# Weight splits and modulation sums on whole pieces of 1024 columns instead of two halves of 512

## The chip, the cores and the metric

One core of a Trainium2 chip runs the whole program. The metric is the device time of one execution in microseconds (us), as the median over several runs of the same kernel. Beside the times there is one profiled execution, from which all rows below come. Engines go by these names: PE is TensorE's matmul, PEld its weight load, DVE VectorE, ACT ScalarE, SP SyncE, which issues the loads of the weights.

## The reference

Two blocks of a network run one after the other over 256 tokens of width 1024, all in fp32. Block 1 has one layer: an attention with low-rank projections beside a pooling branch, a cross attention over a memory, and a mixture of 32 experts. Block 2 has two layers, each with a feed-forward part, a token-mixing part (two kinds of attention, gates and an output product) and a second feed-forward part. Cut to what matters here:

```
mod = silu(c) @ ada_w[l] + ada_b[l]             # nine vectors of 1024 per layer
sh1, sc1, g1, ... = split(mod, 9)
n1 = rms_norm(h, g) * (1 + sc1) + sh1
h  = h + 0.5 * g1 * ((silu(n1 @ wg) * (n1 @ wu)) @ wd)       # feed-forward, d_ff = 2816
```

`c` is one row of 1024 values, so each modulation vector is a matrix of 1024 x 1024 times one vector. `n1 @ wg`, `n1 @ wu` and `@ wd`, and all the projections of the attentions, are dense products of the 256 tokens with a weight matrix.

## The kernel before

**Precision.** The array multiplies in a reduced fp32 form (`float32r`). To keep fp32's accuracy, both factors of a dense product are split in two parts, x = xh + xl and w = wh + wl, and three products are summed: xh wh + xh wl + xl wh (`mm3`, lines 430 to 434). So each weight that is loaded has to go through two elementwise steps before TensorE can use it: ScalarE writes `whi`, the rounded copy (line 205), and VectorE writes `wlo` = w - whi (line 212).

**Pieces.** All weights come from DRAM in pieces of 128 rows x 1024 columns of fp32, 512 KB each (a few are narrower), in the order of their use. The class `Stream` (from line 164) keeps that order. There are three kinds. S is a dense product's weights, split as above: 445 pieces. A is 128 outputs of a modulation vector: 144 pieces (2 layers x 9 vectors x 8). R is the experts' weights, which are used as they come and are not split. `plan` (line 338) places the A pieces among the S pieces; in the phases of block 2 (feed-forward, mixing, feed-forward, for each layer) there are 36, 16, 28, 28, 12 and 8 of them (`ADA_N`, line 43). A feed-forward stage has 66 S pieces: 11 blocks of 256 hidden columns with four pieces of gate and up weights and two of down weights each.

**Slots.** A piece that has been loaded takes one of 4 slots (tag `raw`, tile `w`); the two parts take one of 8 slots each (tags `hi` and `lo`, tiles `whi` and `wlo`). The raw slot is free when VectorE has made `wlo`, or has summed an A piece; the slots of `whi` and `wlo` are free when TensorE has done its last product with the piece. `pump` (line 216) puts out, at each step of the program, all loads, copies and subtractions that the slots allow; a copy comes no sooner than 2 pieces (`LAG`) after its load, a subtraction no sooner than 2 after its copy, unless the piece is due. Each engine runs its instructions in an order that is fixed when the program is built. So a copy that waits for its load holds up everything behind it on ScalarE, and a subtraction everything behind it on VectorE.

**Halves.** `_hi` and `_lo` (lines 199 and 207) work on columns 0 to 511 and 512 to 1023 of a piece in two instructions each. The first half's subtraction needs only the first half's copy. An A piece (`ada_piece`, line 615) is multiplied with the row silu(c) and summed along the columns in two instructions as well: the first starts from the bias and leaves its sum in `apart`, the second starts from `apart` and leaves the result in a column of `acolt`. The products themselves are not wanted and go to `ajunk`, a bf16 tile.

**Gate vectors.** Every third modulation vector is needed along the rows. `ada_finish` (lines 626 to 637) writes it to DRAM by columns (`gate`, line 636) and reads it back to all 128 rows (`growt`, line 637). Both are issued by SyncE, in order with the weights' loads.

**A feed-forward stage** (`ffn`, line 1519). For each block i of hidden columns and each tile t of 128 tokens: `gu_part` multiplies with four pieces; `act` has ScalarE compute `si` = silu(gate) (line 1543) and VectorE the product `pr` (line 1545); `tp` transposes `pr` on TensorE (line 438) and splits it in `hTh` (ScalarE, line 502) and `hTl` (VectorE, line 503); `down` multiplies these with two pieces into `facc`. In TensorE's order, `tp` of block i comes right behind `down` of block i - 1, and `down` of block i one round later.

**Mixing and norms.** In `mix2` (line 1648) two attentions run as units of scores, softmax, transposes and products, with dense products as filler between them. The norms' steps (`NormMod`, from line 2034) run inside the neighbouring products with a raised priority (`urgent`, line 1940), which puts them 30 instructions ahead of where they stand in the program.

The lines that the change and the prediction's steps touch: 205 and 212 (splits), 623 (modulation sums), 192 (loads), 636 and 637 (gates), 502 and 503, 1543 and 1545 (feed-forward), 1736 and 1837 (attention).

Of the kernel before, what the change touches and what calls it, by code (L numbers as in the profile page):

```python
# [10 lines left out]
F32 = mybir.dt.float32  # L11
# [34 lines left out]
# ---------------------------------------------------------------------------  # L46
# constants that depend on shapes alone
# ---------------------------------------------------------------------------
def _constants():
# [4 lines left out]
    # moe: [t', t] = 1 where t' < t  # L54
# [7 lines left out]
    # block 1 attention: chunk mask rows, added as two more rows of the contraction  # L62
# [6 lines left out]
    c["maskrows"] = np.stack([mq, mk], axis=1)  # [2, (q,k), S]  # L69
# [9 lines left out]
    )  # [p, g, t', tok]  # L79
# [3 lines left out]
    # block 2: axial angles, distances  # L83
# [4 lines left out]
    cs = np.stack([np.cos(ang), np.sin(ang)], axis=1).astype(np.float32)  # [S, 2, sec, 16]  # L88
# [8 lines left out]
# ---------------------------------------------------------------------------  # L97
# layout of the inputs
# ---------------------------------------------------------------------------
# [48 lines left out]
class Piece:  # L148
# [7 lines left out]
    def half(self, i):  # L156
        """Columns 512 i to 512 i + 511 of a piece of kind R."""
        if self.tag is None and len(self.place[0]) == 2:
            return self.place[0][i]
        raw = self.place[0][0] if self.tag is None else self.raw  # L160
        return raw[:, i * 512:(i + 1) * 512]


class Stream:
    """The weights in the order of their use: loads run ahead as far as slots are free. Kind S is split
    into two float32r parts ahead of its use; R is used as it is; A goes into a
    modulation vector."""

    def __init__(self, K, order):
        self.K = K  # L170
        self.rec = order is None
        self.order = [] if order is None else order
        self.pos = self.i_dma = self.i_hi = self.i_lo = self.clock = 0
        self.live = {"raw": 0, "hi": 0, "lo": 0}
        self.cap = {"raw": N_RAW, "hi": N_HI, "lo": N_HI}
        self.hold = math.inf  # from this piece on, no splits yet but those that must
        self.extra = []  # more places for pieces of kind R: its tiles, whether it can be used again
        self.deferred = []
        self.ada_done = {}
# [14 lines left out]
    @staticmethod  # L194
    def _halves(p):
        """In two, so that short steps of other chains get in between sooner."""
        return [slice(c, min(c + 512, p.n)) for c in range(0, p.n, 512)]

    def _hi(self, p):
# [4 lines left out]
        for sl in self._halves(p):  # L204
            K.nc.scalar.activation(p.hi[:, sl], p.raw[:, sl], AF.Copy)  # L205

    def _lo(self, p):
# [3 lines left out]
        for sl in self._halves(p):  # L211
            K.nc.vector.tensor_sub(p.lo[:, sl], p.raw[:, sl], p.hi[:, sl].bitcast(F32))  # L212
# [3 lines left out]
    def pump(self, upto=-1, raw=N_RAW):  # L216
        """Puts out the steps that can run by now, and those of the pieces up to a position anyhow."""
# [43 lines left out]
    def hold_after(self, n):  # L261
        """Holds back the splits after those of the next n pieces of kind S."""
# [46 lines left out]
    # modulation vectors: a piece for each 128 rows  # L309
# [28 lines left out]
def plan(order):  # L338
    """Places the pieces of the modulation weights among the others."""
# [11 lines left out]
    at = []  # (position, piece)  # L351
# [7 lines left out]
    # of the others, so many in each phase of the second block: the vector engine has more else to do in some  # L359
# [27 lines left out]
class Kernel:  # L387
# [28 lines left out]
    def load(self, dst, src):  # L416
        """Behind what is traced so far on its queue's engine, so not ahead of weights that are due before."""
        self.tc.keep_in_program_order(self.nc.scalar.dma_start(dst, src))
# [21 lines left out]
    def rsqrt(self, y, v, t, scale, n=1):  # L440
        """y = scale * v ** -0.5 (all [P, n]; t is scratch): a first guess (within 3.4%) from the bits; then
        y <- ((v y^2)^2 + c1 v y^2 + c0) y, the minimax step within that range, which takes b v^-0.5 to
        (b^5 / k) v^-0.5 within 2.6e-5; then Newton's y <- (v y^2 - 3 g^2) y, from g v^-0.5 to -2 g^3 v^-0.5."""
# [20 lines left out]
    def warm(self, n, after=None, tag="mm"):  # L464
        """Products whose results nobody reads, so that the array's clock is not gated down while it has to wait."""
# [14 lines left out]
    def ss(self, dst, src, scale=1.0):  # L480
        """dst [P, 1] = sum of the squares of scale * src (up to 512 columns)."""
# [6 lines left out]
    def rstd(self, st, width, two=True):  # L488
        """(sum of squares / width + eps) ** -0.5 from the sums in st[:, 0:2]."""
# [8 lines left out]
    def split_T(self, hi, lo, src, gain=None):  # L498
        """hi/lo float32r of src * gain, gain per partition."""
# [8 lines left out]
    def transpose_split(self, hi, lo, src, kts, t, k0=0):  # L508
        """hi/lo[:, k0 + k, t's tokens] = src[:, k's columns] ^ T."""
# [29 lines left out]
    def dense(self, name, hi, lo, kt, width, src, evac, cb=512, tag="acc", outer=None, mid=None, pre=None, post=None):  # L539
        """A generator: for each block of columns, out[t] = x[t] @ w, then evac(t, b, out). Groups of  # L540
        outer blocks take all of one tile of tokens before the other; else the tiles take turns at each
        piece. mid follows the first group's first tile; pre(t, b) each evac; post(0)
        precedes the last tile's evac. Yields True between groups."""
# [66 lines left out]
    def c_silu(self):  # L610
        """silu(c) along the rows."""
# [3 lines left out]
    def ada_piece(self, l, m, i, raw):  # L615
        """128 outputs of a vector, by columns, from the transposed weights."""
# [3 lines left out]
        part = self.small(1, "apart")  # L620
        junk = self.ct([P, 512], mybir.dt.bfloat16, name="ajunk")
        for sl, acc, out in ((slice(0, 512), self.gcol("ada_b", (l * 9 + m) * 8 + i), part), (slice(512, D), part, r)):
            self.nc.vector.tensor_tensor_reduce(out=junk, in0=raw[:, sl], in1=self.c_row[:, sl], scale=1.0, scalar=acc,  # L623
                                                op0=ALU.mult, op1=ALU.add, accum_out=out)

    def ada_finish(self, l, m):
# [5 lines left out]
        elif m % 3 == 2:  # L632
            # along the rows, by way of DRAM
# [10 lines left out]
    def gain_row_pe(self, name, tile):  # L644
        """The same without a transfer for each partition; tile() gives places of 512 columns."""
# [15 lines left out]
    # =======================================================================  # L661
# [34 lines left out]
    def mixer(self, nrm):  # L696
# [3 lines left out]
        with self.phase("mix1") as pool:  # L700
# [14 lines left out]
            cs = self.ct([P, 2, 2, 16], name="cs")  # [p, (cos, sin), t, 16]  # L715
            rs = nrm.rs

            def tables():
                """rope tables of the positions"""
# [58 lines left out]
            def rope(x, t, heads, o1, o2):  # L778
                """x: [P, heads, 32] view, in place."""
# [39 lines left out]
            # pooling: d^T = u^T band, y^T = w^T d^T  # L819
# [9 lines left out]
            # gates and the pooling branch run between the steps of the attention  # L829
# [83 lines left out]
            def values(hp, p0, p1):  # L913
# [13 lines left out]
                # transposed, the two heads in their halves of the columns of the array  # L927
# [43 lines left out]
    def cross(self, nrm, pool):  # L971
# [26 lines left out]
        def to_T(dst, src, t, b):  # L998
            """dst[:, 4b.., t] = src ^ T, src [P, 512]."""
# [74 lines left out]
        # what the experts' phase starts with  # L1074
# [16 lines left out]
        # the output product, one tile of tokens after the other; the first two heads' half runs early  # L1091
# [56 lines left out]
    def moe(self, nrm, pool):  # L1148
# [16 lines left out]
        # the weights also use memory that other things need before or later  # L1165
# [20 lines left out]
        def route(t):  # L1186
            """Scores of the groups and experts, the chosen two and their weights."""
# [16 lines left out]
            def first_max(oh, x, n, m):  # L1204
                """oh = 1 at the first of x's greatest, m = the greatest."""
# [18 lines left out]
            # weights: 1 and exp(m2 - m1) over their sum, times 1 / sum of the groups' exponentials  # L1224
# [20 lines left out]
        def rank(t):  # L1245
            """Ranks: earlier tokens of the same expert; beyond 1000 for tokens of others."""
# [34 lines left out]
        # gather: columns of x^T by slot  # L1281
# [4 lines left out]
        def overflow():  # L1286
            # weights of the tokens beyond an expert's slots
# [6 lines left out]
        def gather(q):  # L1294
            """A generator: G and the products of each tile of tokens."""
# [8 lines left out]
            def mm(o, k2, t):  # L1304
                # the bank's first product clears the bits of both halves
# [38 lines left out]
        def slot_weights(q):  # L1344
            """The slots' rows scales, and their weights times these."""
# [14 lines left out]
        # G transposed  # L1360
# [103 lines left out]
    def overflow(self, xnT, cwo, rs, cnti, pool):  # L1464
        """The experts over all tokens, with the weights of those that found no slot; skipped where
        all did."""
# [52 lines left out]
    def ffn(self, l, w, nrm, nxt):  # L1519
        nc, S_ = self.nc, self.S  # L1520
        A, V, T = nc.scalar, nc.vector, nc.tensor
        with self.phase(f"ffn{l}{w}") as pool:
# [53 lines left out]
            # the first two and the last take all of one tile of tokens before the other  # L1576
# [71 lines left out]
    def mix2(self, l, nrm, nxt):  # L1648
# [3 lines left out]
        with self.phase(f"mix2{l}") as pool:  # L1652
# [26 lines left out]
            def tables():  # L1679
                """The distances and slopes; the cosines and sines with the gains (and the scale of the scores)."""  # L1680
# [44 lines left out]
            def rope(out, o, n, t, j):  # L1725
                """out = the rotated heads of o (PSUM) with their gains, not yet normalized; the sums of squares."""
# [457 lines left out]
```

## Time and profile before

| | before |
|---|---|
| runs: median (lowest to highest of 3) | 1723.43 us (1722.06 to 1725.42) |
| profiled execution: span from its first to its last instruction | 1710.4 us |
| around the span, to the runs' median | 13.0 us |
| instructions: copies `whi`, subtractions `wlo` | 888 and 888 |
| instructions: modulation sums | 288, each with a read of the accumulator |
[...]

The profiled execution's own time is told as its span; the runs are timed around it, so the 13.0 us are what lies before the first and after the last instruction. The profile's page gives busy time for each engine. Its views group instructions by line, list what each engine waited for (`A <- B`: A sat idle until B was done), and give the busy time in stretches of the span. The stretches used below: block 1's attentions 0 to 300 us, the experts 300 to 525, then block 2: feed-forward 535 to 735, mixing 735 to 945, feed-forward 945 to 1130 and 1130 to 1335, mixing 1335 to 1505, feed-forward 1505 to 1695.

### The profile page before, as it was taken

The numbers are of one execution on the slowest core, as the hardware profiler recorded it, in microseconds if no ns is written. First come the engines' busy times: TensorE is split into PE (matmuls) and PEld (weight loads), VectorE is DVE, ScalarE is ACT, GpSimd is POOL, SyncE is SP. The second block draws the span as 40 slices with busy tenths as digits, with TensorE's granted clock in tenths as the row PEclk, the third lists the DMA queues.
The fourth block names the chain that finished last, engine by engine and source line by source line (L and its number), as shares of the span: only waits on it lengthen the run. The fifth ranks groups of instructions, "written<-read, shape, count | busy, mean of one in ns | idle before, by whom it ended". The sixth has DMA issues, their size and how long they took to land.

```text
span 1710.4 us, 22657 instructions
## 1 busy us (share of the span) xinstructions
PE 1600.0 (94%) x7704; PEld 1197.0 (70%) x7704; DVE 1139.6 (67%) x2633; ACT 817.2 (48%) x1752; POOL 0.2 (0%) x4
## 2 busy tenths in 40 slices
PE   8999999788879989889999899999998999999998
PEld 7878887333115767667778787877876877878886
DVE  7878756111008878687889777778775788886664
ACT  5655642111006434366765444455443768474442
POOL 0000000000000000000000000000000000000000
PEclk9999999989999999999999999999999999999999
DMA  7667759799996898755576887858787744756663
GB/s 247 206 216 280 231 181 360 273 409 408 408 408 222 302 262 289 248 197 196 167 239 199 254 283 256 273 183 301 257 267 184 222 166 160 244 185 212 223 211 89
DMA packets 128645, 424.10 MB, mean 248 GB/s; under 512 B 21098, under 2 KB 23434, under 8 KB 128524
## 3 DMA queue, kind: packets, MB, share of 16 engines
q1 hardware_dynamic: 122160, 414.00, 70.5%
q10 hardware_dynamic: 6364, 8.60, 1.7%
q8 instruction: 62, 1.02, 0.2%
q14 instruction: 59, 0.48, 0.1%
HBM read 421.47 MB, written 1.07 MB: 247 GB/s over the span
## 4 chain that ended last, share of the span: by engine, by line
PE 33%; DMA 29%; DVE 11%; ACT 3%; issue 3%; SPq 0%; DVEq 0%; ACTq 0%
DMA w<-in_w_dram 19%; DMA w<-in_wm_dram 6%; DVE wlo L212 5%; PE d L432 4%; PE d L434 4%; PE d L433 4%; PE ps L433 3%; PE ps L434 3%; PE ps L432 3%; DVE ajunk L623 3%; PE ps L438 2%; DMA gate<-acolt 2%; PE facc L432 2%; PE facc L433 2%; PE facc L434 2%
## 5 line engine op out<-in xcount | busy, mean ns | idle before, releaser
L205 ACT ACTIVATE whi<-w 128x512 fp32r<-128x512 f32 (+1 forms) x888 | 513.6, 622 | 460.3 <-DMA w<-in_w_dram 314.3
L212 DVE TENSOR_TENSOR wlo<-w,whi 128x512 fp32r<-128x512 f32 (+1 forms) x888 | 574.3, 682 | 159.9 <-ACT whi L205 156.3
L432 PE MATMUL ps<-whi,xh 128*128 128x512 f32 x704 | 278.8, 396 | 0.8 <-ACT xh L2080 0.5
L433 PE MATMUL ps<-wlo,xh 128*128 128x512 f32 x704 | 275.3, 391 | 0.8 <-DVE wlo L212 0.7
L434 PE MATMUL ps<-whi,xl 128*128 128x512 f32 x704 | 275.1, 391 | 0.0
L432 PE MATMUL d<-whi,xh 128*128 128x512 f32 (+3 forms) x528 | 206.4, 391 | 0.2 <-ACT xh L2080 0.2
L433 PE MATMUL d<-wlo,xh 128*128 128x512 f32 (+3 forms) x528 | 203.5, 385 | 1.1 <-DVE stat L457 1.1
L434 PE MATMUL d<-whi,xl 128*128 128x512 f32 (+3 forms) x528 | 203.2, 385 | 1.0 <-DVE xl L503 1.0
L623 DVE CUSTOM_DVE_ANT_0 ajunk<-w,c_row,cols 128x512 bf16<-128x512 f32 x144 | 107.5, 746 | 95.5 <-DMA w<-in_w_dram 95.5
L433 PEld LDWEIGHTS ps<-wlo,xh 128*128 128x128 f32 x704 | 132.5, 188 | 28.2 <-DVE wlo L212 2.0
L432 PEld LDWEIGHTS ps<-whi,xh 128*128 128x128 f32 x704 | 132.4, 188 | 28.0 <-ACT xh L2080 1.2
L434 PEld LDWEIGHTS ps<-whi,xl 128*128 128x128 f32 x704 | 132.3, 188 | 28.0 <-DVE xl L2081 0.4
L432 PE MATMUL facc<-whi,hTh 128*128 128x512 f32 x352 | 144.9, 412 | 4.4 <-ACT hTh L502 4.4
L434 PE MATMUL facc<-whi,hTl 128*128 128x512 f32 x352 | 140.7, 400 | 1.1 <-DVE hTl L503 1.0
L433 PE MATMUL facc<-wlo,hTh 128*128 128x512 f32 x352 | 140.9, 400 | 0.0
L432 PEld LDWEIGHTS d<-whi,xh 128*128 128x128 f32 x528 | 100.2, 190 | 21.2 <-issue 3.6
L434 PEld LDWEIGHTS d<-whi,xl 128*128 128x128 f32 x528 | 100.3, 190 | 20.1 <-DVE xl L503 1.7
L433 PEld LDWEIGHTS d<-wlo,xh 128*128 128x128 f32 x528 | 100.4, 190 | 18.4 <-DVE wlo L212 1.7
L623 DVE CUSTOM_DVE_ANT_0 ajunk<-w,c_row,apart 128x512 bf16<-128x512 f32 x144 | 107.7, 748 | 3.1
L1399 PE MATMUL ps<-w,xg 128*32 128x512 f32 x472 | 86.3, 623 | 14.3 <-DMA w<-in_wm_dram 7.9
L432 PEld LDWEIGHTS facc<-whi,hTh 128*128 128x128 f32 x352 | 68.3, 194 | 19.4 <-ACT hTh L502 6.6
L434 PEld LDWEIGHTS facc<-whi,hTl 128*128 128x128 f32 x352 | 68.0, 193 | 17.3 <-DVE hTl L503 2.6
(405 smaller groups left out, 1855.2 us busy)
## 6 DMA issues: line engine op xcount, KB each, us to landing
w<-in_w_dram SPq DMA_DIRECT2D x578, 512.0 KB, 4.5
w<-in_wm_dram SPq DMA_DIRECT2D x163, 512.0 KB, 9.3
adaacc<-in_wm_dram SPq DMA_DIRECT2D x16, 512.0 KB, 10.2
xf<-in_wm_dram SPq DMA_DIRECT2D x16, 256.0 KB, 9.6
growt<-gate SPq DMA_DIRECT2D x6, 512.0 KB, 5.7
w<-in_w_dram SPq DMA_DIRECT2D x6, 384.0 KB, 3.7
growt<-in_rows_dram ACTq DMA_DIRECT2D x4, 512.0 KB, 6.0
bg<-in_rows_dram ACTq DMA_DIRECT2D x8, 256.0 KB, 4.7
```

The source lines that it names most:

```text
L205: K.nc.scalar.activation(p.hi[:, sl], p.raw[:, sl], AF.Copy)
L212: K.nc.vector.tensor_sub(p.lo[:, sl], p.raw[:, sl], p.hi[:, sl].bitcast(F32))
L432: mm(out, lhsT=xh, rhs=wh, start=start, stop=False)
L433: mm(out, lhsT=xh, rhs=wl, start=False, stop=False)
L434: mm(out, lhsT=xl, rhs=wh, start=False, stop=stop)
L438: self.nc.tensor.transpose(out, in_, self.ident[:k, :k])
L623: self.nc.vector.tensor_tensor_reduce(out=junk, in0=raw[:, sl], in1=self.c_row[:, sl], scale=1.0, scalar=acc, op0=ALU.mult, op1=ALU.add, a ...
L1399: T.matmul(gu[e * CAP:(e + 1) * CAP, :], lhsT=xg[j // 2][:, k, c:c + CAP], rhs=p.half(e % 2), start=(k == 0), stop=(k == KD - 1), tile_pos ...
```

## The change

A piece's copy is one instruction over all its columns, and its subtraction another; `_halves` is gone. An A piece is summed in one instruction that starts from the bias and leaves its result in the column of `acolt`. Its products, in fp32, overwrite the piece itself; `ajunk` and `apart` are gone. All comments are taken out as well.

```diff
-    @staticmethod
-    def _halves(p):
-        return [slice(c, min(c + 512, p.n)) for c in range(0, p.n, 512)]
...
     def _hi(self, p):
...
         p.hi = K.wpool.tile([P, PIECE], F32R, name="whi", tag="hi", bufs=N_HI)
-        for sl in self._halves(p):
-            K.nc.scalar.activation(p.hi[:, sl], p.raw[:, sl], AF.Copy)
+        K.nc.scalar.activation(p.hi[:, :p.n], p.raw[:, :p.n], AF.Copy)
 
     def _lo(self, p):
...
         p.lo = K.wpool.tile([P, PIECE], F32R, name="wlo", tag="lo", bufs=N_HI)
-        for sl in self._halves(p):
-            K.nc.vector.tensor_sub(p.lo[:, sl], p.raw[:, sl], p.hi[:, sl].bitcast(F32))
+        K.nc.vector.tensor_sub(p.lo[:, :p.n], p.raw[:, :p.n], p.hi[:, :p.n].bitcast(F32))
...
     def ada_piece(self, l, m, i, raw):
...
         r = self.ada_accs[(l, m)][:, i:i + 1]
-        part = self.small(1, "apart")
-        junk = self.ct([P, 512], mybir.dt.bfloat16, name="ajunk")
-        for sl, acc, out in ((slice(0, 512), self.gcol("ada_b", (l * 9 + m) * 8 + i), part), (slice(512, D), part, r)):
-            self.nc.vector.tensor_tensor_reduce(out=junk, in0=raw[:, sl], in1=self.c_row[:, sl], scale=1.0, scalar=acc,
-                                                op0=ALU.mult, op1=ALU.add, accum_out=out)
+        self.nc.vector.tensor_tensor_reduce(out=raw, in0=raw, in1=self.c_row, scale=1.0,
+                                            scalar=self.gcol("ada_b", (l * 9 + m) * 8 + i),
+                                            op0=ALU.mult, op1=ALU.add, accum_out=r)
```

## Rows read from the trace of the kernel before

**Rows 1.** The page, part 1: engine, busy us (share of span), instructions.

```profile
PE 1600.0 (94%) x7704; PEld 1197.0 (70%) x7704; DVE 1139.6 (67%) x2633; ACT 817.2 (48%) x1752; POOL 0.2 (0%) x4
```

**Rows 2.** What TensorE waited for: us in total, times, longest us.

```profile
PE ps L438 <- DVE pr L1545: 35.4, 14, 6.6
...
PE ps L433 <- DVE wlo L212: 0.7, 2, 0.5
```

**Rows 3.** Stretches: length; busy us of PE, PEld, DVE, ACT, POOL; clock; DMA share; GB/s.

```profile
600.00:735.00 135.00, 115.80 (x500) 92.73 (x500) 95.71 (x210) 51.07 (x103) 0.00 (x0) 0.95 0.83 267
...
1548.00:1677.00 129.00, 129.00 (x584) 106.30 (x583) 76.65 (x145) 60.48 (x120) 0.00 (x0) 1.00 0.66 202
```

**Rows 4.** What ScalarE waited for from 600 to 735 us.

```profile
ACT whi L205 <- DMA w<-in_w_dram: 69.0, 30, 9.4
```

**Rows 5.** Loads of weights from 600 to 735 us: count, KB each, us to landing.

```profile
w<-in_w_dram SPq DMA_DIRECT2D x65, 512.0 KB, 5.0
```

**Rows 6.** What SyncE's queue waited for from 600 to 735 us.

```profile
SPq L637 <- DMA gate<-acolt: 17.9, 2, 9.3
```

**Rows 7.** A stretch behind the first long wait; columns as in rows 3.

```profile
616.80:623.50 6.70, 4.20 (x11) 3.43 (x12) 6.10 (x13) 3.14 (x8) 0.00 (x0) 0.50 0.87 303
```

**Rows 8.** Groups by line and shape: count, busy us, mean ns, idle before.

```profile
L205 ACT ACTIVATE whi<-w 128x512 fp32r<-128x512 f32 x877 | 510.0, 625 | 459.9 <-DMA w<-in_w_dram 313.9 <-PE ps L434 47.2 <-PE facc L434 34.8
...
L205 ACT ACTIVATE whi<-w 128x256 fp32r<-128x256 f32 x6 | 2.4, 404 | 0.0
...
L212 DVE TENSOR_TENSOR wlo<-w,whi 128x512 fp32r<-128x512 f32 x877 | 570.0, 685 | 159.9 <-ACT whi L205 156.3 <-PE d L434 0.9
...
L623 DVE CUSTOM_DVE_ANT_0 ajunk<-w,c_row,cols 128x512 bf16<-128x512 f32 x144 | 107.5, 746 | 95.5 <-DMA w<-in_w_dram 95.5
...
L994 DVE TENSOR_TENSOR mem<-mem,growt 128x1024 f32<-128x1024 f32 x2 | 2.4, 1217 | 0.0
```

**Rows 9.** Timeline, one S piece: start, length, engine, line, count, [idle before].

```profile
646.84 1.15 ACT L205 ACTIVATE whi<-w 128x512 fp32r<-128x512 f32 x2 [2.51 <-DMA w<-in_w_dram]
...
647.50 1.29 DVE L212 TENSOR_TENSOR wlo<-w,whi 128x512 fp32r<-128x512 f32 x2 [0.84 <-ACT whi L205]
```

**Rows 10.** Timeline of VectorE ahead of a late `pr`: sum, subtraction, `pr`.

```profile
1047.26 0.75 DVE L623 CUSTOM_DVE_ANT_0 ajunk<-w,c_row,cols 128x512 bf16<-128x512 f32 x1 [1.78 <-DMA w<-in_w_dram]
...
1048.74 1.29 DVE L212 TENSOR_TENSOR wlo<-w,whi 128x512 fp32r<-128x512 f32 x2
...
1049.94 0.75 DVE L1545 TENSOR_TENSOR pr<-ps,si 128x256 f32<-128x256 f32 x2
```

**Rows 11.** The same ahead of another: two pieces' copies, then `pr`.

```profile
615.67 2.43 ACT L205 ACTIVATE whi<-w 128x512 fp32r<-128x512 f32 x4 [3.65 <-DMA w<-in_w_dram]
...
618.83 0.42 DVE L1545 TENSOR_TENSOR pr<-ps,si 128x256 f32<-128x256 f32 x1
```

**Rows 12.** The same ahead of a third: half a copy, then `pr`.

```profile
655.46 0.63 ACT L205 ACTIVATE whi<-w 128x512 fp32r<-128x512 f32 x1 [2.82 <-DMA w<-in_w_dram]
...
656.72 0.42 DVE L1545 TENSOR_TENSOR pr<-ps,si 128x256 f32<-128x256 f32 x1
```

**Rows 13.** Timeline of ScalarE at a feed-forward stage's end.

```profile
1126.03 0.63 ACT L205 ACTIVATE whi<-w 128x512 fp32r<-128x512 f32 x1 [2.28 <-DMA w<-in_w_dram]
1126.56 0.36 ACT L502 ACTIVATE hTh<-ps 128x256 fp32r<-128x256 f32 x1
```

**Rows 14.** Timeline of VectorE in the mixing: a lone half, then `zqa`.

```profile
806.58 0.68 DVE L212 TENSOR_TENSOR wlo<-w,whi 128x512 fp32r<-128x512 f32 x1
807.18 0.68 DVE L1736 TENSOR_TENSOR zqa<-zqa,rtmp 128x512 f32<-128x512 f32 x1
```

**Rows 15.** A stretch, columns as in rows 3; then `ajunk`'s instructions alone (DVE).

```profile
903.00:946.00 43.00, 42.96 (x204) 34.74 (x203) 39.90 (x92) 26.94 (x55) 0.00 (x0) 1.00 0.62 197
...
903.00:946.00 43.00, 7.45 (x10) 1.00 0.62 197
```

## The prediction, made before the changed kernel was run

> **What bounds the kernel now.** I read the page's busy shares first. TensorE is busy for 1600.0 of 1710.4 us and VectorE for 1139.6 [rows 1], so only about 110 us of the span are TensorE's to win, and VectorE is no bound on average. The list of what TensorE waited for then says which engine's lateness matters: the splits themselves almost never do (0.7 us on `wlo` in the whole span), while the transposes of the gated products `pr` waited 35.4 us in 14 places [rows 2]. All 14 lie in the four feed-forward stages of block 2. The busy time by stretch shows that a stage can also be free of any stall: from 1548 to 1677 us TensorE is busy all 129 us, whereas from 600 to 735 it is idle for 19 us [rows 3]. In that second stretch ScalarE's splits stood 69.0 us waiting for weights [rows 4], so the stream of weights is late there, and `pr` is late only because its `si` and its own product stand behind late splits in two in-order queues. Two things make the stream late. A piece's slot (four of them) is filled again only after VectorE has read it, and a load takes 5.0 us [rows 5]; and SyncE, which issues the loads, stood 17.9 us waiting for the gate vectors' scatter before it could go on [rows 6]. [...]
>
> So what is to be asked of this change is not how much busy time it saves, but how long a chain takes from a landed piece to a free slot and to `pr`.
>
> **Prices of the new instructions.** The copy on ScalarE takes 625 ns for 512 columns and 404 for 256 [rows 8], 221 ns for 256 more, so 625 + 2 x 221 = 1067 ns for 1024 (an estimate). On VectorE a two-operand step over 1024 columns is in the trace: 1217 ns against 685 for 512 [rows 8], 532 ns more. The modulation sum over 512 columns takes 746 ns [rows 8]; with 532 more a whole one takes 1.28 us. That it writes fp32 in place instead of bf16 into a junk tile shows in no row; I take nothing for it, since 512 columns take 532 ns in the step that writes fp32 too; at worst it is another 0.5 us on each of 144, 77 us of VectorE's time, at best nothing.
>
> In a queue the start to the next start counts. A lone half holds VectorE for 0.60 us (806.58 to 807.18) [rows 14], 0.085 less than its duration, so a whole subtraction holds it for 1.13 us against 1.20 for two halves: 0.07 saved on each of 443 pieces that have two halves, 31 us in all. The two halves of a sum hold it for 1.48 us (1047.26 to 1048.74) [rows 10], a whole one for 1.28 - 0.07 = 1.21: 0.27 saved 144 times, 39 us. ScalarE saves about 0.08 a piece, 35 us. None of these 105 us lies on the path by itself; TensorE's work covers them, and the instructions, loads and their queue are otherwise unchanged: one load a piece as before, no wait added.
>
> [...]
>
> **1. From landing to a free slot.** Now: a copy starts at 646.84, its first half releases the subtraction at 647.50, which ends 1.29 us later [rows 9], 1.95 us in all. Two engines work on two halves at once. With whole pieces the subtraction can only start when all of the copy is done: 1.067 + 0.03 + 1.217 = 2.31 us, 0.36 more. A modulation piece is free 0.27 us earlier. From 600 to 735 us, 65 loads [rows 5] in 135 - 17.9 us are 1.80 us a load, so 7.2 us a slot, of which 5.0 are the load. With about two split pieces to one modulation piece (66 to 36 in this stage's order) the round gets (2 x 0.36 - 0.27) / 3 = 0.15 us longer, 0.037 us a load: +2.4 us for 65. Ends: 0 if loads get faster because fewer are in flight; +5.9 if the sums always stand behind a longer subtraction (0.36 on each). I take +2.4: that is what the chains give without either. In the other feed-forward stages part of the copies wait for slots of `whi` that TensorE frees, so the longer chain is covered; without that cover the 2 x 94 loads of the next two stages (66 split pieces and 28 modulation pieces each) would cost +7.0.
>
> **2. From landing to `pr`.** With today's order kept, the 14 waits end as follows. Five have a sum and then both halves of a subtraction ahead of `pr` [rows 10]: 0.27 + 0.07 earlier, -1.7 us. Five have two pieces' copies and subtractions ahead [rows 11]: the second subtraction can't begin at its copy's middle, some +0.3 each, +1.5. One has a copy's half, `si`, a subtraction's half, `pr` [rows 12]: `si` fits between the halves now, and later `pr` would start at 655.46 + 1.067 + 0.03 + 1.13 = 657.69 instead of 656.72, +0.97. Two have half a sum or half a subtraction ahead, where a whole one would be, +0.9; one stands behind a backlog, -0.1. At the stages' ends three transposed products `hTh` stand behind one half of a copy [rows 13], +0.43 each, +1.3, and one behind a sum, -0.3. Sum +2.6. Ends: -3 if the new order puts `pr` ahead of the subtractions, +7 if it always comes behind.
>
> **3. Attention.** Three of TensorE's waits there stand behind a lone half of a subtraction, as `zqa` does [rows 14]. A whole one in its place holds VectorE 1.13 instead of 0.60 us: 3 x 0.53 = +1.6. At best the split moves behind the step, -1.8; the other end is the second rival.
>
> **4. Lead before a gate's transfer.** From 903 to 946 us VectorE is busy for 39.90 of 43 us, five sums among that [rows 15] (ten halves). There its speed does set how far the splits run ahead of TensorE when SyncE next stalls. Five sums save 1.3 us: -1.3, between 0 and the first rival.
>
> Sum: 2.4 + 2.6 + 1.6 - 1.3 = +5.3 us on the profiled span of 1710.4, 1715.7. The runs' median is 1723.43, 13.0 us above the span for what lies around it, so **1728.7 us**, 0.3% slower. A measurement of this kernel can tell about 0.2%, 3.4 us, from no change.
>
> **Rivals.** *VectorE's relief becomes lead: faster.* 70 us less on VectorE let the splits run one piece further ahead before the gates' transfers. A piece is 12 matmuls at 129 / 584 = 0.22 us [rows 3], 2.65 us; at the three transfers where copies wait for loads rather than for slots that is -8.0, and one half-clock stretch less [rows 7] is another -3.4: 1712 to 1715, I say 1714. For it: VectorE at 93% in rows 15. Against it: from 600 to 735 VectorE is busy for 95.7 of 135 us [rows 3], so it is latency and not its rate that holds the lead there.
>
> *Short steps wait behind whole pieces: slower still.* Norms, softmax and rotation alternate between ScalarE and VectorE. About 18 attention units in blocks 1 and 2 and 18 norm chains each put a result before TensorE; if half a split more, 0.53 us, stood ahead of each and nothing filled TensorE in that time, it would be 36 x 0.53 = 19 us, 1742. It decides where a chain has less than 0.5 us of slack. Against it: the filler products between those steps.
>
> *It cancels.* Ends of points 1 to 3 of both signs lie within a few us, and a stage like 1548 to 1677 [rows 3] can't gain or lose: 1723.5.
>
> **How the numbers follow.** Forecast 0.36 (a little of it, 0.02, within 0.2%), short steps 0.16, cancelling 0.26, relief 0.22. So slower 0.50, same 0.28, faster 0.22. The range goes from 1713, near the relief case, to 1744, a little above the short steps: about 2 in 10 lie outside, mostly the lower half of the relief and orders of the queues that I don't foresee. The forecast's own range is 1725 to 1736.
>
> **What would show it.** Copies of about 1.07 us and subtractions of about 1.22 us, 445 each; 144 sums of about 1.28 us; VectorE's busy time down by some 70 us and TensorE's idle time nonetheless up by about 5; the wait on `pr` at 36 to 40 us; in 600 to 735 about 1.84 us a load outside the gates' holes. The step is wrong if the wait on `pr` falls below 30 us (relief), or if new waits of 0.5 us appear in attention and norms (short steps); the whole is wrong if a sum in place takes much more than 1.3 us.

## The result, and the profile after

| | before | after |
|---|---|---|
| median (lowest to highest of 4 runs) | 1722.74 us (1721.93 to 1725.42) | 1737.94 us (1735.46 to 1740.37) |
| ratio after / before | | 1.0103 (95% interval 1.0073 to 1.0132) |
| span of the profiled execution | 1710.4 us | 1735.6 us |
| mean granted clock of TensorE, as a share of full speed | 0.982 | 0.976 |

The changed kernel is 1.0% slower, some 15 us by the medians. The forecast was 0.3% slower, 5.3 us: the sign held, the size was a third of what came. 1737.94 lies inside the range of 1713 to 1744, and 2 us above the forecast's own 1725 to 1736. The two spans differ by more than the medians, 25.2 us. The execution that was profiled after took 1737.35 us, 1.75 more than its span; with as much around it the profiled execution before took about 1712 us (an estimate), some 10 below its median. So stage by stage the two profiles show up to 10 us more than the runs do.

Page part 1 of the changed kernel: busy us of each engine, share of the span, instructions.

```profile
PE 1606.5 (93%) x7704; PEld 1200.9 (69%) x7704; DVE 1085.6 (63%) x1902; ACT 779.8 (45%) x1309; POOL 0.2 (0%) x4
```

Against [rows 1] VectorE has 54.0 us less to do and ScalarE 37.4 (817.2 to 779.8). TensorE does the same 7704 matmuls, and takes 6.5 us longer for them; the rest of the 25.2 us, 18.7, is idle time of TensorE. The groups by line and shape (line 199 is the copy, 205 the subtraction, 613 the sum):

```profile
L205 DVE TENSOR_TENSOR wlo<-w,whi 128x1024 fp32r<-128x1024 f32 x434 | 527.0, 1222 | 185.5 <-ACT whi L199 182.1 <-PE d L427 0.6
L199 ACT ACTIVATE whi<-w 128x1024 fp32r<-128x1024 f32 x434 | 458.9, 1059 | 477.6 <-DMA w<-in_w_dram 255.5 <-PE d L427 85.9 <-PE ps L427 56.0
...
L613 DVE CUSTOM_DVE_ANT_0 w<-w,c_row,cols 128x1024 f32<-128x1024 f32 x144 | 184.7, 1282 | 136.8 <-DMA w<-in_w_dram 136.1
```

1222, 1059 and 1282 ns stand against 1217, 1067 and 1278 in the prediction: the prices were right, and a sum in place costs nothing extra. So the loss is not in what the instructions take. What TensorE waited for, in us, times and longest us:

```profile
PE ps L431 <- DVE pr L1536: 34.6, 12, 9.0
PE facc L425 <- ACT hTh L495: 10.5, 3, 7.1
...
PE ps L425 <- ACT xh L2071: 6.6, 3, 3.4
...
PE ps L431 <- DVE zqa L1727: 3.1, 2, 1.7
PE d L425 <- ACT xh L2071: 2.7, 3, 1.7
...
PE ps L431 <- DVE p L1828: 1.9, 2, 1.6
```

The wait on `pr` is where it was [rows 2]. The new one is on `xh`, the first operand that a norm in block 2 hands to the next products: 9.3 us in 6 places, where before it was 0.7 us in two.

### The profile page after: what moved, and what is told of

Its sections match the earlier page's. It is cut to its first block, busy times and chain, and to the rows that moved or that the text cites. A ratio compares the mean times of both kernels' runs of the same rounds, so it can differ in the third digit from the quotient of the medians.

```text
span 1735.6 us, 21452 instructions
## 1 busy us (share of the span) xinstructions
PE 1606.5 (93%) x7704; PEld 1200.9 (69%) x7704; DVE 1085.6 (63%) x1902; ACT 779.8 (45%) x1309; POOL 0.2 (0%) x4
## 4 chain that ended last, share of the span: by engine, by line
DMA 32%; PE 28%; DVE 11%; issue 5%; ACT 5%; SPq 0%; DVEq 0%; ACTq 0%
DMA w<-in_w_dram 22%; DMA w<-in_wm_dram 5%; DVE wlo L205 5%; DMA gate<-acolt 3%; PE d L425 3%; PE d L427 3%; PE d L426 3%; ACT whi L199 3%; PE ps L426 2%; PE ps L427 2%; PE ps L425 2%; DVE w L613 2%; PE ps L431 2%; PE ps L1390 2%; PE facc L425 2%
## 5 line engine op out<-in xcount | busy, mean ns | idle before, releaser
L199 ACT ACTIVATE whi<-w 128x1024 fp32r<-128x1024 f32 (+2 forms) x445 | 467.3, 1052 | 486.4 <-DMA w<-in_w_dram 264.4
L205 DVE TENSOR_TENSOR wlo<-w,whi 128x1024 fp32r<-128x1024 f32 (+2 forms) x445 | 536.3, 1213 | 187.4 <-ACT whi L199 184.0
L613 DVE CUSTOM_DVE_ANT_0 w<-w,c_row,cols 128x1024 f32<-128x1024 f32 x144 | 184.7, 1282 | 136.8 <-DMA w<-in_w_dram 136.1
L425 PE MATMUL facc<-whi,hTh 128*128 128x512 f32 x352 | 145.9, 414 | 10.5 <-ACT hTh L495 10.5
L426 PEld LDWEIGHTS facc<-wlo,hTh 128*128 128x128 f32 x352 | 69.2, 197 | 13.4
```

What stands on the lines that cost most here:

```text
L199: K.nc.scalar.activation(p.hi[:, :p.n], p.raw[:, :p.n], AF.Copy)
L205: K.nc.vector.tensor_sub(p.lo[:, :p.n], p.raw[:, :p.n], p.hi[:, :p.n].bitcast(F32))
L425: mm(out, lhsT=xh, rhs=wh, start=start, stop=False)
L426: mm(out, lhsT=xh, rhs=wl, start=False, stop=False)
L613: self.nc.vector.tensor_tensor_reduce(out=raw, in0=raw, in1=self.c_row, scale=1.0, scalar=self.gcol("ada_b", (l * 9 + m) * 8 + i), op0=ALU ...
```

## Where the time went: a norm at the end of a mixing stage

At the end of `mix2` the norm's scaled rows `xs` are transposed on TensorE; ScalarE and VectorE make `xf`, then ScalarE `xh`; the next feed-forward stage's first product `ps` reads that. While this goes on, TensorE works off products `d` that are still left of the mixing. The timeline of the kernel before there, all engines but the weight loads:

```profile
925.74 0.93 PE L438 MATMUL ps<-cst,xs 128*128 128x128 f32 x7
...
926.95 1.48 ACT L2075 ACTIVATE xf<-ps,acolt 128x128 f32<-128x128 f32 x4
...
928.32 0.64 ACT L205 ACTIVATE whi<-w 128x512 fp32r<-128x512 f32 x1
...
928.84 1.15 ACT L2080 ACTIVATE xh<-xf 128x512 fp32r<-128x512 f32 x2
...
930.16 0.39 PE L432 MATMUL ps<-whi,xh 128*128 128x512 f32 x1
```

and of the kernel after:

```profile
936.04 1.06 PE L431 MATMUL ps<-cst,xs 128*128 128x128 f32 x8
...
937.67 1.06 ACT L199 ACTIVATE whi<-w 128x1024 fp32r<-128x1024 f32 x1 [1.87 <-DMA w<-in_w_dram]
...
938.64 1.49 ACT L2066 ACTIVATE xf<-ps,acolt 128x128 f32<-128x128 f32 x4
...
940.01 1.06 ACT L199 ACTIVATE whi<-w 128x1024 fp32r<-128x1024 f32 x1
940.96 1.15 ACT L2071 ACTIVATE xh<-xf 128x512 fp32r<-128x512 f32 x2
...
941.64 0.50 PE L425 MATMUL ps<-whi,xh 128*128 128x512 f32 x1 [3.39 <-ACT xh L2071]
```

Two things have changed. On ScalarE a whole copy stands between `xf` and `xh` where half a copy stood, and another, waiting 1.87 us for its load, stands ahead of `xf`. And TensorE has less left to do meanwhile. The products `d` alone, from the end of the transposes to the first `ps` (length, busy us, count, clock, DMA share, GB/s), before and after:

```profile
926.67:930.16 3.49, 3.49 (x16) 1.00 0.64 215
```

```profile
937.16:941.64 4.48, 1.10 (x5) 1.00 0.86 310
```

Before, the first half of `xh` was there at about 929.4 and its reader came at 930.16, 0.7 us to spare. Sixteen products have become five: in the order of TensorE's instructions, which is fixed when the program is built, the transposes now stand 11 products later. Of the 3.39 us of idle time, 2.4 are the 11 products (3.49 - 1.10), the rest the longer chain, less what was to spare. Most of the longer chain is the copy ahead of `xf`, which starts 1.5 us behind the end of the transposes instead of 0.3; the whole copy in place of a half adds 0.5. The next layer's mixing ends in the same way, 16 products before (from 1510.3) and 5 after, and 2.87 us of wait at 1529.28. Each wait is followed by a stretch at half the clock, 0.51 and 0.50 (columns as in [rows 3]):

```profile
1529.20:1532.60 3.40, 3.32 (x8) 2.66 (x9) 3.34 (x5) 0.54 (x2) 0.00 (x0) 0.51 0.64 254
942.20:945.50 3.30, 3.30 (x9) 2.63 (x8) 3.30 (x6) 1.07 (x2) 0.00 (x0) 0.50 0.39 150
```

At half the clock the products there start 0.43 us apart, against 3.49 / 16 = 0.22 for the products `d` of before, at clock 1.00. So 3.4 us hold 1.7 us of work (an estimate from the clock), and such a boundary costs 3 + 1.7, nearly 5 us.

## The experiments

Each was timed in alternation with the kernel before on the same chip; the ratio is to that. The last column is TensorE's wait on `xh` behind the norms of block 2.

| kernel | median us | ratio (95% interval) | span us | wait on `xh`, us |
|---|---|---|---|---|
| `sums` | 1735.48 | 1.0106 (1.0081 to 1.0130) | 1730.9 | 0.7 |
| `splits` | 1750.22 | 1.0177 (1.0150 to 1.0204) | 1753.4 | 6.9 |
| `copy` | 1741.53 | 1.0133 (1.0106 to 1.0160) | 1740.5 | 4.9 |
| `sub` | 1741.47 | 1.0140 (1.0113 to 1.0168) | 1738.4 | 5.5 |
| `uneven` | 1717.91 | 0.9985 (0.9963 to 1.0006) | 1716.0 | 0.7 |
| `after_again` | 1742.64 | 1.0112 (1.0081 to 1.0144) | 1739.2 | 9.7 |
| `gates_pool_before` | 1715.04 | 0.9956 (0.9936 to 0.9976) | 1718.8 | 0.7 |
| `gates_pool_after` | 1737.92 | 1.0088 (1.0061 to 1.0116) | 1733.1 | 10.1 |
| `pg_before` | 1696.77 | 0.9842 (0.9813 to 0.9872) | 1686.7 | 0.7 |
| `pg_after` | 1713.47 | 0.9945 (0.9921 to 0.9968) | 1708.8 | 9.8 |
| `mix_halves` | 1735.59 | 1.0064 (1.0042 to 1.0086) | 1739.1 | 4.0 |
| `mix_whole` | 1730.85 | 1.0044 (1.0020 to 1.0067) | 1720.9 | 5.9 |

### The change in parts

`sums` takes only the modulation sums whole, `splits` only the two steps of the splits, `copy` only ScalarE's step, `sub` only VectorE's. For `copy` the edit is

```diff
-        for sl in self._halves(p):
-            K.nc.scalar.activation(p.hi[:, sl], p.raw[:, sl], AF.Copy)
+        K.nc.scalar.activation(p.hi[:, :p.n], p.raw[:, :p.n], AF.Copy)
```

and the others take the other lines of the change in the same way.

> The kernel before, with only the modulation sums on whole pieces (in place, fp32); the splits stay in halves. Theory 1 (the longer chain of a whole split is what costs): the sums are the gain in the change, so 0 to 6 us faster than before, 1717 to 1723 us. Theory 2 (a whole sum blocks VectorE for 1.2 us and the short steps wait behind it): 5 to 12 us slower, 1728 to 1735. Theory 3 (where SyncE's fixed order puts the read-back of a gate decides): at the last gate no load stands between scatter and read-back in this program, as in the changed one, so TensorE stalls there for 5 to 7 us, where before it did not, whatever the sums give: about 1728.

> The kernel before, with only the splits (copy and subtraction) on whole pieces; the sums stay in halves. Theory 1: all of the loss and what the sums gave back, +15 to +20 us, 1738 to 1743. Theory 2: little, 0 to +5 us. Theory 3: two loads stand between scatter and read-back of the last gate here, so its stall of 6 us is gone; about +8, 1731.

> The kernel before, with only ScalarE's copies on whole pieces; subtractions and sums in halves. Theory 1: the first subtraction can't start at the middle of the copy, the chain from a landed piece to its free slot gets 0.4 us longer, and steps of ScalarE (norms' xf and xh, hTh, si) wait behind a whole copy: +8 to +12 us, most of the loss. Theory 2: 0 to +3. Theory 3: the last gate has no load between, +6 there alone.

> The kernel before, with only VectorE's subtractions on whole pieces; copies and sums in halves. Theory 1: the subtraction has to wait for both halves of the copy, so the chain gets about as long as with whole copies (1.15 + 0.03 + 1.22 = 2.4 us against 1.95), but ScalarE's short steps still get in between halves: +4 to +10 us. Theory 2: 0 to +3. Theory 3: the gates have loads between as before, no stall of that kind: about +3.

Every part alone costs about as much as all together, or more, and the parts don't add: 1.06% and 1.77% for sums and splits, 1.0 to 1.1% for both. By the ratios, all four lost more than any of the theories allowed, by 6 to 14 us. The last column parts them. Wherever a step of the splits is whole, TensorE waits 4.9 to 6.9 us on `xh`, and at the two mixing stages' ends 9 products (`copy` and `sub`, both ends) or 7 and 5 (`splits`) cover the norm; with sums alone all 16 are there and the wait is 0.7 us as before. So the norms' lost cover comes from the splits, and already from one of their two steps. It is not all that a whole step costs: of the feed-forward stages' waits, that on `pr` is longer in `copy`, and that on `hTh` in `splits` (35.4 [rows 2] and 4.4 us before):

```profile
PE ps L437 <- DVE pr L1544: 48.6, 19, 9.1
```

```profile
PE facc L430 <- ACT hTh L500: 14.9, 4, 6.2
```

So in these profiles the chains that the prediction's term 2 is about do get later with one whole step alone. The sums' own loss is something else than the norms' cover. What TensorE waited for in `sums`:

```profile
PE ps L438 <- DVE pr L1543: 27.8, 10, 7.3
PE facc L432 <- ACT hTh L502: 12.5, 3, 8.5
```

The two together are 40.3 us, against 35.4 [rows 2] and 4.4 before. But for the same 7704 matmuls TensorE was busy 1612.5 us instead of 1600.0, at a mean granted clock of 0.972 instead of 0.982. So more than half of the 20.5 us that the span grew is clock, not waiting. By stages, 8.4 us of the 20.5 lie in the last feed-forward stage (175.2 to 183.6). There theory 3 held, if with a shorter stall: no load stands between the last gate's scatter and its read-back, SyncE stood 9.8 us, and TensorE waited 3.72 us for `pr`, with half the clock behind it (products 0.43 us apart). Another 6.3 us lie in the first mixing stage (193.7 to 200.0), at a granted clock of 0.98 instead of 1.00. Two waits of TensorE stand there:

```profile
770.23 0.50 PE L434 MATMUL d<-whi,xl 128*128 128x512 f32 x1 [2.06 <-DVE xl L2079]
804.55 0.74 PE L438 MATMUL ps<-cst,p 128*128 128x128 f32 x4 [3.01 <-DVE p L1835]
```

On VectorE `xl` and `p` came right behind a whole sum of 1.28 us that had itself waited 2.07 and 1.62 us for its load. Of the rest, 6.6 us lie in block 1's attentions and were not followed. Why the sums cost nothing more once the splits are whole stays open.

### Was the order before merely lucky?

Any edit of these lines shifts the orders in which the engines run. `uneven` keeps two instructions a step, but cuts pieces at 480 columns, which shifts the orders without making a piece whole.

```diff
-        return [slice(c, min(c + 512, p.n)) for c in range(0, p.n, 512)]
+        return [slice(0, 480), slice(480, p.n)] if p.n > 480 else [slice(0, p.n)]
```

> The kernel before, with the splits' halves cut at column 480 instead of 512 (480 and 544 columns): as many instructions and as much work as before, but the planned order of the queues moves: some 300 of VectorE's 2693 instructions, 84 of ScalarE's and 154 of TensorE's stand elsewhere. Theory 1 (length of the chains): within 3 us of before. Theory 4 (the order of before is a lucky one, and any change of it costs about 1%, which is why each of the four parts alone was as slow as all together): 10 to 25 us slower.

> The change itself once more, on the same chip as its neighbours, so that they can be compared. Every theory: 0.7 to 1.4% slower than before, with the sums' and splits' parts alone not below it.

`uneven` took the time of before (0.9985); the change itself came out at 1.0112 beside it. So not every shift of the order costs 1%. But it is one control, and a mild one: counted in the traces, by tiles and shapes, as the fewest of the 7704 matmuls that have to be moved to get from one order to the other, 85 moved in `uneven`, 116 in `sums` and 254 in the change. That a shift as large as the change's would cost nothing without whole pieces isn't shown.

### The gates

The prediction put the holes in the stream of weights down to SyncE, which waits for a gate's scatter before it issues more loads. Here GpSimd issues both transfers instead:

```diff
-            nc.sync.dma_start(d.rearrange("(k p) -> p k", p=P), col)
-            nc.sync.dma_start(r, d.unsqueeze(0).to_broadcast([P, D]))
+            nc.gpsimd.dma_start(d.rearrange("(k p) -> p k", p=P), col)
+            nc.gpsimd.dma_start(r, d.unsqueeze(0).to_broadcast([P, D]))
```

> The kernel before, with the gate vectors' scatter and read-back issued by GpSimd instead of SyncE, so that the loads of the weights are never held up by them. Theory 3 (holes behind the gates): the five long waits behind gates, about 25 us of TensorE's idle time and the half-clock stretches after them, go: 15 to 30 us faster, about 1690 to 1708. If other waits take their place: within 5 us of before.

> The change, with the gates issued by GpSimd. Theory 3: without the holes the change is within 4 us of the kernel before with the gates on GpSimd. Theory 1 (chains and short steps behind whole pieces): the change remains 8 to 15 us slower than that kernel, and the waits on xh at the stages' starts remain.

The kernel before won only 0.4%, and the change still cost 1.3% (1.0088 / 0.9956). Its wait on `pr` stayed at 33.8 us in 17 places, although SyncE no longer waits. So SyncE's wait is at most a small part of what makes the holes. The transfers in the kernel before, from 596 to 608 us, while a gate is scattered (packets by size, then loads: count, KB each, median us to landing):

```profile
DMA packets 1507, 1.73 MB, mean 144 GB/s; under 512 B 1089, under 2 KB 1089, under 8 KB 1505
...
w<-in_w_dram SPq DMA_DIRECT2D x2, 512.0 KB, 11.6
gate<-acolt SPq DMA_DIRECT2D x1, 4.0 KB
```

1089 of 1507 packets are under 512 B (96 in the same window without a scatter, below): the 1024 values of the gate go out nearly one by one, the window moves 144 GB/s, and the two loads issued right behind the scatter land after 11.6 us instead of 5.0 [rows 5]. So the next pair makes the row on TensorE: a diagonal of the gate's columns, times a matrix of ones, copied from PSUM; nothing goes by way of DRAM.

```diff
-            d = self.dram.tile([D], F32, name="gate", tag="gate", bufs=2)
...
-            nc.sync.dma_start(d.rearrange("(k p) -> p k", p=P), col)
-            nc.sync.dma_start(r, d.unsqueeze(0).to_broadcast([P, D]))
+            for b in range(2):
+                xf = self.ct([P, 4, P], name="xf", tag="xf", bufs=2)
+                nc.vector.tensor_tensor(xf, self.ident.unsqueeze(1).to_broadcast([P, 4, P]),
+                                        col[:, 4 * b:4 * b + 4].unsqueeze(2).to_broadcast([P, 4, P]), op=ALU.mult)
+                o = self.ps("tr")
+                nc.tensor.matmul(o, lhsT=self.ones, rhs=xf.rearrange("p k c -> p (k c)"), start=True, stop=True)
+                nc.scalar.activation(r[:, b * 512:(b + 1) * 512], o, AF.Copy)
```

> The kernel before, with the six gate rows made on TensorE (a diagonal of the gate's columns times a matrix of ones, copied from PSUM) instead of written to DRAM by elements of 4 bytes and read back. No load then stands behind a scatter. If the scatter's transfer is what holds the loads up, the five long waits at the gates (some 25 us) and the half clock behind them (some 14 us) go: 1685 to 1705 us, ratio 0.98 to 0.99. If SyncE's waiting was the whole cause, it equals the kernel with the gates issued by GpSimd (1715, 0.996). If the waits only move to the next shortage of loads: same.

> The change, whole, on the kernel with the gate rows made on TensorE. Theory A (the short steps of norms and of the softmax wait behind whole pieces, and the splits' chain is longer; gates have no part): 12 to 22 us over its own base, as with the gates in place. Theory B (whole pieces cost little by themselves; what costs is that with them the loads are fewer pieces ahead when a gate holds them up): within 6 us of its base.

`pg_before` is 1.6% faster than the kernel before, 26 us, as the first theory said, and the fastest of all kernels here. In the same window, 596 to 608 us:

```profile
DMA packets 914, 3.37 MB, mean 281 GB/s; under 512 B 96, under 2 KB 96, under 8 KB 912
...
w<-in_w_dram SPq DMA_DIRECT2D x7, 512.0 KB, 5.2
```

The edit takes the read-back from DRAM away together with the scatter; which of the two the 26 us belong to was not parted. And yet the change costs on this kernel what it cost with the gates in place: 0.9945 / 0.9842 is 1.0105, 16.7 us by the medians. So theory A holds as to the total: the loss needs no gates. The places differ, though: in the pair with the gates, 11.7 of the 25.2 us between the spans lie in the two mixing stages and 9.2 in the last feed-forward stage, behind the last gate. This pair shows the loss most clearly. TensorE's waits on `pr` and `xh` in `pg_before`

```profile
PE ps L438 <- DVE pr L1548: 12.5, 13, 2.2
```

```profile
PE ps L432 <- ACT xh L2083: 0.5, 1, 0.5
...
PE d L432 <- ACT xh L2083: 0.2, 1, 0.2
```

and in `pg_after`

```profile
PE ps L436 <- DVE pr L1544: 12.9, 10, 2.8
PE ps L430 <- ACT xh L2079: 7.1, 4, 3.3
...
PE d L430 <- ACT xh L2079: 2.7, 3, 1.7
```

and the two mixing stages, from the last `pr` of one feed-forward stage to the first of the next (columns as in [rows 3]), in `pg_before`

```profile
730.90:923.80 192.90, 187.42 (x970) 149.70 (x970) 160.31 (x392) 127.44 (x299) 0.00 (x0) 1.00 0.60 201
...
1302.70:1496.10 193.40, 187.64 (x972) 149.94 (x970) 155.13 (x372) 130.04 (x303) 0.00 (x0) 1.00 0.58 192
```

and in `pg_after`:

```profile
736.10:937.40 201.30, 191.81 (x966) 150.94 (x966) 158.63 (x311) 125.46 (x249) 0.00 (x0) 0.98 0.63 204
...
1317.10:1517.60 200.50, 191.42 (x966) 151.64 (x965) 152.58 (x299) 125.18 (x249) 0.00 (x0) 0.98 0.60 192
```

They are 8.4 and 7.1 us longer, 15.5 of the 22.1 between the spans (1686.7 and 1708.8; the medians differ by 16.7). Idle time grew by 4.0 and 3.3 us, busy time by 4.4 and 3.8. Most of the latter is the half clock, which was nowhere in these stages and now is in each of them twice, for about 3.4 us that hold 1.7 us of work:

```profile
792.30:795.80 3.50, 3.50 (x13) 2.33 (x13) 2.48 (x4) 1.09 (x6) 0.00 (x0) 0.51 0.80 259
1352.00:1355.50 3.50, 3.50 (x11) 2.84 (x11) 2.10 (x4) 3.45 (x5) 0.00 (x0) 0.52 0.77 241
```

```profile
928.90:932.30 3.40, 2.98 (x7) 2.40 (x8) 3.13 (x6) 1.95 (x3) 0.00 (x0) 0.50 0.88 325
1509.10:1512.50 3.40, 3.05 (x7) 2.47 (x8) 3.07 (x5) 0.82 (x2) 0.00 (x0) 0.51 0.75 283
```

The second pair follows the norm at the stage's end, where 2.67 and 3.31 us of idle time came in, with 5 products as cover for what 16 covered (in `pg_before`, from 912.8):

```profile
925.54:929.32 3.78, 1.12 (x5) 0.94 0.87 292
```

The first pair lies inside the attention, behind waits of 2.19 and 2.02 us. These are the second rival's own case, a short step behind a whole piece:

```profile
789.53 1.28 DVE L618 CUSTOM_DVE_ANT_0 w<-w,c_row,cols 128x1024 f32<-128x1024 f32 x1 [1.00 <-DMA w<-in_w_dram]
790.75 0.48 DVE L1836 SCALAR_TENSOR_TENSOR p<-p,mx 128x256 f32<-128x256 f32 x1
791.28 0.44 PE L436 MATMUL ps<-cst,p 128*128 128x128 f32 x2 [2.19 <-DVE p L1836]
```

```profile
1350.25 1.06 ACT L204 ACTIVATE whi<-w 128x1024 fp32r<-128x1024 f32 x1 [3.77 <-DMA w<-in_w_dram]
1351.21 0.58 ACT L1712 ACTIVATE z<-d 128x512 f32<-128x512 f32 x1
1351.85 0.88 PE L436 MATMUL ps<-cst,z 128*128 128x128 f32 x4 [2.02 <-ACT z L1712]
```

In both the whole piece had waited for its load as well, so the wait is the late load's and the piece's length together; which share is which was not tested.

### Halves in some stages only

`mix_halves` keeps halves for splits and sums while `mix2` is written out, and takes whole pieces elsewhere; `mix_whole` is its complement. The test `self.halve` stands at the three places of the change:

```diff
-        for sl in self._halves(p):
+        for sl in self._halves(p) if self.halve else [slice(0, p.n)]:
...
+            self.S.halve = True
             nrm = self.mix2(l, nrm, lambda: NormMod(self, l, 2))
+            self.S.halve = False
```

> The change in all stages but the two attention stages of block 2, which keep halves for splits and sums. Theory A with its main place there (the profiled stages between about 744 to 938 and 1329 to 1522 us were 7.5 and 4.1 us longer after the change): these stages come back to 194 and 193 us, and the whole is 8 to 12 us below the change, 1726 to 1730. If the loss is made by the state in which loads stand when such a stage begins, they stay longer, and the whole stays at 1736 to 1742.

> The complement: whole pieces in the two attention stages of block 2 alone, halves elsewhere. Theory A with its main place there: 8 to 12 us over the kernel before (ratio 1.005 to 1.007), and with the kernel that has halves there the two add up to the change's 15. If each stage's loss comes from elsewhere: within 3 us of the kernel before.

The two losses add up: 0.64% and 0.44%, 1.08% together. Their place is less sharp than I expected: `mix_halves` took 1735.6 us, not 1726 to 1730. `mix_halves` waits 4.0 us on `xh`, and its mixing stages have 9 products of cover at both ends, neither 16 nor 5; in its profile they took 197.8 and 198.1 us, not the 194 and 193 that I expected. `mix_whole` waits 5.9 us, with 7 and 9 products. So whole pieces outside the mixing take part of its cover away too.

## Why the prediction was right in sign, and short in size

**Prices**: right to 8 ns, and VectorE is relieved by 54 us of the 70 forecast (what makes the difference was not followed). **The relief becomes lead** (first rival): refuted. No kernel with a whole step was faster than the one with the same gates and halves throughout. A whole subtraction does take less than two halves, 1222 ns against two of 685, and that saves nothing here, since that time is off the path.

**1, from landing to a free slot (+2.4)**: the chain is longer as worked out, but the stream is not slower. Shifted by the 3 us that the stage begins later, from 603 to 738 us, these are the loads and SyncE's wait:

```profile
w<-in_w_dram SPq DMA_DIRECT2D x65, 512.0 KB, 4.8
```

```profile
SPq L628 <- DMA gate<-acolt: 19.5, 2, 10.1
```

(135 - 19.5) / 65 is 1.78 us a load, where I expected 1.84 and had 1.80 before. The lower end that I gave, faster loads, came: 4.8 us instead of 5.0.

**2, from landing to `pr` (+2.6)** and **3, attention (+1.6)**: both near nothing in the changed kernel. The wait on `pr` is 34.6 us against 35.4, in the pair without scatters 12.9 against 12.5. (The 14 waits before lie in three of the four feed-forward stages, 7, 4 and 3 of them, and not in all four, as the prediction has it.) That on `hTh` grew from 4.4 to 10.5, but 7.1 of it is one wait behind a gate; without the scatters it is 2.3 us against 1.5. In attention the waits on `zqa` and `p` together are 5.0 us against 5.9.

**4, lead before a gate (-1.3)**: no gain is seen. The last feed-forward stage, which I had held for unable to lose [rows 3], became 9.2 us longer in the profile (175.2 to 184.4): in the changed order no load stands between the last gate's scatter and its read-back, where one stood before. SyncE stood 11.3 us there, against 8.7, and TensorE 6.25 at 1699.6, against nothing. Without scatters that stage costs 177.8 against 177.2 us.

**The right sign is in good part luck.** Of the four terms that gave it, none shows at its size, and the loss came by a way that the sum put at nothing.

**The step that failed** is the one that says "With today's order kept". All four terms move durations within the order of before. Each size was reckoned on a chain's neighbours, and the orders changed. The second rival had the right mechanism, short steps behind whole pieces, at 0.53 us in each of 36 places; I held against it "the filler products between those steps". It was that filler that went: at two norms 11 of 16 products, 2.4 us each, with a whole copy inside the chain and a half-clock stretch behind. The sign that the prediction gave for this rival, new waits in the norms, came: 9.3 us on `xh`. Its 19 us came nearer than my 5.3, though from a few large waits and not from many small ones. At nearly 5 us each the two norms make up some 10 of the 15 us; where the rest lies differs between the pairs with and without gates. Why the builder writes the transposes later when pieces are whole was not tested, nor was a kernel with whole pieces and the old cover: that the lost cover makes these waits is read from the traces.

**Around the span**: 13.0 us were taken from one execution's span and other executions' median. It is about 1.75 us, so what lies before the first and after the last instruction is not 13.0 us; the rest is that one execution, faster than the median.

## What to carry to other kernels

Merging instructions on engines that are off the critical path bought nothing here, and made each of them a longer obstacle for the short steps that are on it. Before pricing such a change, look at every hand-over between stages for how many products cover it: a cover with 0.7 us to spare can go with a shift of the order, and a hole of 3 us cost half as much again in clock. If small values have to be turned from columns to rows, try it on the array before a scatter to DRAM and a read-back: here that gave 1.6%.

## What the runs showed that I had not expected

Around a scatter of 4 KB, the 1024 values of a gate, the loads are late: they land after 11.6 us instead of 5.2 (596 to 608 us), and where GpSimd issues the scatter after 13.3 (592 to 605 us). Six such gates, scatter and read-back together, cost this kernel 26 us. Half-clock stretches (clock 0.52 and 0.51, in `pg_after`) followed single waits as short as 2.02 and 2.19 us. And of two edits, each of which costs over 1% alone, the second may cost less than nothing once the first is there: whole sums make the kernel with halves 1.06% slower, and the kernel with whole splits is slower without them than with them (1.0177 against 1.0112 and 1.0103).
